# Strassen's seven products for the first block's gate and up products

## The chip, the cores and the metric

The program runs on one core of one Trainium2 chip. The metric is the device time of one execution, in microseconds (us). The engines are TensorE (PE in the profile; PEld are its weight loads), VectorE (DVE), ScalarE (ACT), GpSimd (POOL) and SyncE (SP), which starts the DMAs here.

## The reference

Two transformer-like blocks of depth 2 each, one after the other, on 512 tokens of 1024 features; the first block puts 16 more tokens in front (528). All is float32. What the change touches is the feed-forward part of the first block's two layers, cut here from the reference:

```python
        hn = rms_norm(h, norm_ffn_g[l])
        g, u = jnp.split(hn @ w_gu[l], [D_FF], axis=-1)
        h = h + (jax.nn.silu(g) * u) @ w_down[l]
```

with 1024 features and `D_FF` = 2816. Ahead of it in a layer stands the mixer (attention and a recurrent branch, joined by an output product), behind the second layer stands the second block.

## The kernel before, in words

Features lie on the partitions, in tiles of 128: the residual `h` is 8 tiles of 128 x 528 float32. Nothing is multiplied in plain float32: both operands are split into a high part (rounded to fp32r) and the rest, and a product is three matmuls, high by high, high by low and low by high (`mm3`, L95 to L98). A moving operand in two parts is `xa` (`xh_all`, `xl_all`). A weight tile of 1024 x 128 arrives by DMA as `wraw`; `weight` (L86 to L93) makes `whi` with a ScalarE cast (L90) and `wlo` with a VectorE subtraction (L92), three buffers of each. `split` (L120) does the same for an activation (L121 ScalarE, L122 VectorE).

The feed-forward part of a layer is L571 to L603. `prep` (L256) scales `h` by the norm's gain and writes it to `xa` in two parts (L260 ScalarE, L261 VectorE); the norm's factor per token, `r2`, comes from `sumsq` (L180, adds at L186) and `rnorm` (L153), and is multiplied in after the products. The 22 tiles of gate features and the 22 of up features are done pair by pair, in groups of 8, 7 and 7 pairs (`nf`). A pair is: 8 tiles of K times three matmuls over all the tokens for the gate (`proj`, L111), eviction times `r2` (L588, VectorE), silu (L589, ScalarE), the same for up (L593), their product (L594, VectorE) and its split into `yh` and `yl` (L121, L122). The tokens are two spans of 264 in layer 0 and one of 512 in layer 1, where the 16 extra tokens are no longer needed. After a group, its part of the down product goes through 8 tiles of output features `m`, summed over the group's `nf` tiles, and is added to `h` (L602).

The mixer ends with the output product `w_out` (L551), whose second half (n = 1) is added to `h[m]` for m = 0 to 7 in turn (L561); `prep` follows tile by tile. GpSimd has no instruction in the feed-forward part. In other stages it adds squares and sums (L680, L692), multiplies by rope tables (L401, L652), adds to `h` in the mixer (L559) and squares (L1106).

PSUM is one pool for the whole program: 8 banks, named mm (3), sc (2), tr, av and bc. The framework that builds the program puts each engine's instructions in an order of its own making (ready ones first, by their place in the program), and sets the semaphores; on the chip every engine runs its queue in order.

## Time and profile before

| | us |
|---|---|
| median of 3 runs | 2864.72 |
| lowest, highest | 2864.29, 2868.45 |
| span of the profiled execution | 2861.2 |
| TensorE busy in it | 2781.5 (97%) |
| VectorE busy | 1736.3 (61%) |
| ScalarE busy | 1227.4 (43%) |
| GpSimd busy | 367.0 (13%) |

A page of the profile is read from its first part (busy times) to the chain that ended last (part 4), which says on which engine the time was spent; the granted clock (PEclk) is TensorE's, as a share of its full 2.4 GHz. Matmuls are pipelined: one shows about 0.28 us, though the next starts after 0.12 us, so their cost is the distance between starts. An operation on DVE or POOL shows its own time and any time in which it had started but could not go on.

### The profile page before, as it was taken

The numbers are of one execution on the slowest core, as the hardware profiler recorded it, in microseconds if no ns is written. First come the engines' busy times: TensorE is split into PE (matmuls) and PEld (weight loads), VectorE is DVE, ScalarE is ACT, GpSimd is POOL, SyncE is SP. The second block draws the span as 40 slices with busy tenths as digits, with TensorE's granted clock in tenths as the row PEclk, the third lists the DMA queues.
The fourth block names the chain that finished last, engine by engine and source line by source line (L and its number), as shares of the span: only waits on it lengthen the run. The fifth ranks groups of instructions, "written<-read, shape, count | busy, mean of one in ns | idle before, by whom it ended". The sixth has DMA issues, their size and how long they took to land.

```text
span 2861.2 us, 42993 instructions
## 1 busy us (share of the span) xinstructions
PE 2781.5 (97%) x16548; PEld 2422.5 (85%) x16548; DVE 1736.3 (61%) x3534; ACT 1227.4 (43%) x2174; POOL 367.0 (13%) x403
## 2 busy tenths in 40 slices
PE   8989999999999999999999999999999999999998
PEld 7989999999887888887889888888877898888887
DVE  7887434457888434458977573333789875633335
ACT  6665222235665222235665442332445754433323
POOL 0011000000110000002220031111322110311112
PEclk9999999999999999999999999999999999999999
DMA  4332332332333333336324123333264242233331
GB/s 146 89 79 85 90 89 85 94 89 92 99 85 100 95 92 94 94 95 166 112 82 140 59 81 97 96 96 96 70 155 132 75 136 72 60 106 95 96 96 64
DMA packets 96491, 277.18 MB, mean 97 GB/s; under 512 B 13344, under 2 KB 20000, under 8 KB 96288
## 3 DMA queue, kind: packets, MB, share of 16 engines
q1 hardware_dynamic: 96288, 274.45, 32.7%
q8 instruction: 131, 2.15, 0.3%
q14 instruction: 72, 0.59, 0.1%
HBM read 241.82 MB, written 2.10 MB: 85 GB/s over the span
## 4 chain that ended last, share of the span: by engine, by line
PE 87%; DVE 8%; issue 2%; ACT 2%; POOL 1%; DMA 1%; SPq 0%; ACTq 0%; DVEq 0%; POOLq 0%
PE mm L97 25%; PE mm L98 25%; PE mm L96 25%; PE av L96 1%; PE av L97 1%; PE av L98 1%; PE av L161 1%; DVE wlo L92 1%; PE bc L827 1%; PE av L712 1%; PE tr L827 1%; DVE sq L402 1%; PE bc L176 0%; PE sc L96 0%; PE sc L833 0%
## 5 line engine op out<-in xcount | busy, mean ns | idle before, releaser
L96 PE MATMUL mm<-xh_all,whi 128*128 128x512 f32 (+2 forms) x2752 | 926.0, 338 | 12.4 <-ACT xh_all L260 6.8
L97 PE MATMUL mm<-xl_all,whi 128*128 128x512 f32 (+2 forms) x2752 | 930.3, 339 | 1.4 <-DVE xl_all L745 0.8
L98 PE MATMUL mm<-xh_all,wlo 128*128 128x512 f32 (+2 forms) x2752 | 925.9, 337 | 0.0
L90 ACT CAST whi<-wraw 128x1024 fp32r<-128x1024 f32 (+2 forms) x460 | 465.4, 1013 | 1017.7 <-PE mm L97 823.9
L92 DVE TENSOR_TENSOR wlo<-wraw,whi 128x1024 fp32r<-128x1024 f32 (+2 forms) x437 | 540.7, 1238 | 233.7 <-ACT whi L90 231.7
L96 PEld LDWEIGHTS mm<-xh_all,whi 128*128 128x128 f32 x2752 | 518.8, 189 | 66.6 <-ACT xh_all L260 6.8
L97 PEld LDWEIGHTS mm<-xl_all,whi 128*128 128x128 f32 x2752 | 519.8, 189 | 54.5 <-DVE xl_all L745 1.8
L98 PEld LDWEIGHTS mm<-xh_all,wlo 128*128 128x128 f32 x2752 | 521.0, 189 | 49.8
L1106 POOL TENSOR_TENSOR r<-r 128x512 f32<-128x512 f32 (+1 forms) x70 | 101.9, 1456 | 531.6 <-ACT r L1105 531.6
L97 PE MATMUL mm<-yl,whi 128*128 128x264 f32 (+1 forms) x528 | 169.9, 322 | 0.1
L98 PE MATMUL mm<-yh,wlo 128*128 128x264 f32 (+1 forms) x528 | 169.5, 322 | 0.0
L96 PE MATMUL mm<-yh,whi 128*128 128x264 f32 (+1 forms) x528 | 168.5, 320 | 0.0
L673 DVE TENSOR_TENSOR hall<-hall,mm 128x512 f32<-128x512 f32 (+1 forms) x82 | 46.6, 568 | 145.9 <-PE mm L98 145.9
L593 DVE TENSOR_TENSOR su<-mm,rbc 128x264 f32<-128x264 f32 (+1 forms) x66 | 34.3, 519 | 139.8 <-PE mm L98 139.8
L602 DVE TENSOR_TENSOR hall<-hall,mm 128x264 f32<-128x264 f32 (+1 forms) x72 | 37.1, 515 | 120.6 <-PE mm L98 120.6
L97 PEld LDWEIGHTS mm<-yl,whi 128*128 128x128 f32 x528 | 99.2, 188 | 8.8 <-DVE yl L122 0.6
L96 PEld LDWEIGHTS mm<-yh,whi 128*128 128x128 f32 x528 | 99.0, 188 | 7.6
L98 PEld LDWEIGHTS mm<-yh,wlo 128*128 128x128 f32 x528 | 99.2, 188 | 7.3
L588 DVE TENSOR_TENSOR sg<-mm,rbc 128x264 f32<-128x264 f32 (+1 forms) x66 | 34.0, 517 | 103.2 <-PE mm L98 101.6
L671 DVE SCALAR_TENSOR_TENSOR hall<-hall,mm 128x512 f32<-128x512 f32 x32 | 22.0, 687 | 66.9 <-PE mm L98 66.8
L692 POOL TENSOR_TENSOR accq<-accq,nsq 128x512 f32<-128x512 f32 (+1 forms) x48 | 57.9, 1205 | 25.4 <-ACT nsq L690 24.0
L432 POOL MEMSET vh<- 128x128 f32 x8 | 1.6, 205 | 463.6 <-PE mm L98 414.8
(672 smaller groups left out, 5446.3 us busy)
## 6 DMA issues: line engine op xcount, KB each, us to landing
wraw<-w2f SPq DMA_DIRECT2D x128, 512.0 KB, 3.7
wraw<-w1gu SPq DMA_DIRECT2D x88, 512.0 KB, 3.6
wraw<-w2in SPq DMA_DIRECT2D x44, 512.0 KB, 3.9
wraw<-w1in SPq DMA_DIRECT2D x40, 512.0 KB, 3.7
wraw<-w2mkv SPq DMA_DIRECT2D x32, 512.0 KB, 3.8
wraw<-w1dn SPq DMA_DIRECT2D x32, 448.0 KB, 3.3
wraw<-w1out SPq DMA_DIRECT2D x32, 256.0 KB, 2.7
wraw<-w1dn SPq DMA_DIRECT2D x16, 512.0 KB, 3.5
```

The costliest lines, as they stand in the source:

```text
L90: nc.scalar.copy(hi[:, :kt], raw[:, :kt])
L92: (eng or nc.vector).tensor_sub(lo[:, :kt], raw[:, :kt], f(hi[:, :kt]))
L96: nc.tensor.matmul(ps, wh, xh, start=first, stop=False)
L97: nc.tensor.matmul(ps, wh, xl, start=False, stop=False)
L98: nc.tensor.matmul(ps, wl, xh, start=False, stop=last)
L588: nc.vector.tensor_mul(sg[:, a:b], p, r2[:, a:b])
L593: nc.vector.tensor_mul(su[:, a:b], p, r2[:, a:b])
L602: nc.vector.tensor_add(h[m][:, a:b], h[m][:, a:b], p)
L673: nc.vector.tensor_add(X(m, a, b), X(m, a, b), p)
L692: nc.gpsimd.tensor_add(self.accq[:, a:b], self.accq[:, a:b], sq[:, a:b])
L827: nc.tensor.transpose(ps[:, 128 * j:128 * j + 128], p[:, 128 * j:128 * j + 128], ident)
L1106: nc.gpsimd.tensor_mul(r[:, a:b], r[:, a:b], r[:, a:b])
```

## The change

The products of a pair of weight tiles, `w1` (gate) and `w2` (up), become seven products of quarters in place of eight. The two halves of K (4 tiles each) are one pair of indices, gate and up another, and the first and second half of the tokens the third. `halves4` makes four sums and differences of 4-tile halves of the weights on GpSimd (two tiles of scratch, `s` and `s4`, one buffer each), and splits the seven halves in two parts. The moving side's sums and differences are made once a layer, in the place of `prep` (three GpSimd and one VectorE operation of half the tokens for each of 4 pairs of feature tiles). `seven` runs the products, each 4 tiles of K times three matmuls over half the tokens (264 or 256 columns), and adds them up in four VectorE operations from PSUM to `e`. `r2` is now multiplied in on GpSimd, before and after the silu. The groups are 6, 6, 5 and 5 pairs. The down product goes over the tokens in halves in both layers, with one eviction for both. PSUM is now a pool that is closed and opened anew at the start and the end of each feed-forward part, with three pairs of banks inside it. All else in the diff is comments taken out.

```diff
+    def halves4(pool, w1, w2):
+        r1 = wpool.tile([128, 8, 128], F32, name="wraw", bufs=3)
+        nc.sync.dma_start(r1, w1)
+        r2 = pool.tile([128, 8, 128], F32, name="wraw2", bufs=2)
+        nc.sync.dma_start(r2, w2)
+        s = pool.tile([128, 8, 128], F32, name="ws", bufs=1)
+        s4 = pool.tile([128, 4, 128], F32, name="ws4", bufs=1)
+        nc.gpsimd.tensor_add(s[:, 4:], r2[:, :4], r2[:, 4:])
+        nc.gpsimd.tensor_sub(s[:, :4], s[:, 4:], r1[:, :4])
+        nc.gpsimd.tensor_sub(r2[:, :4], r1[:, :4], r2[:, :4])
+        nc.gpsimd.tensor_sub(s4, r1[:, 4:], s[:, :4])
+        got = []
+        for x in (r1, s, r2, s4):
+            if x is s4:
+                hi = pool.tile([128, 4, 128], F32R, name="wh4", bufs=1)
+                lo = pool.tile([128, 4, 128], F32R, name="wl4", bufs=1)
+            else:
+                hi = wpool.tile([128, 8, 128], F32R, name="whi", bufs=3)
+                lo = wpool.tile([128, 8, 128], F32R, name="wlo", bufs=3)
+            split(hi, lo, x)
+            got += [(hi[:, o:o + 4], lo[:, o:o + 4]) for o in range(0, hi.shape[1], 4)]
+        return got
+    def seven(pool, w, x, n):
+        a11, a12, s2, s1, s3, a22, s4 = w
+        b11, b21, t2, t1, t3, b22, t4 = x
+        def product(ps, w, x):
+            for k in range(4):
+                mm3(ps, w[0][:, k], w[1][:, k], x[0][k], x[1][k], k == 0, k == 3)
+        e = pool.tile([128, 4, n], F32, name="quarters", bufs=2)
+        u = pool.tile([128, n], F32, name="u1", bufs=2)
+        p1 = bank("av")[:, :n]
+        p26, p57, p34 = (pair_of_banks()[:, :, :n] for _ in range(3))
+        product(p1, a11, b11)
+        nc.scalar.copy(u, p1)
+        product(p26[:, 0], a12, b21)
+        product(p26[:, 1], s2, t2)
+        nc.vector.tensor_add(e[:, 0:4:3], p26, twice(u))
+        product(p57[:, 0], s1, t1)
+        product(p57[:, 1], s3, t3)
+        nc.vector.tensor_add(e[:, 1:3], p57, twice(e[:, 3]))
+        nc.vector.tensor_add(e[:, 3], p57[:, 0], e[:, 2])
+        product(p34[:, 0], s4, b22)
+        product(p34[:, 1], a22, t4)
+        nc.vector.tensor_add(e[:, 1:3], p34, e[:, 1:3])
+        return e
...
-                prep(G_FFN, l0, T)
+                half = (T - l0) // 2
+                n0, n1 = slice(l0, l0 + half), slice(l0 + half, T)
+                th, tl = (ff.tile([128, 4, 3, half], F32R, name=n) for n in ("th", "tl"))
+                with tc.tile_pool(name="tq", bufs=1, side="right") as tq:
+                    for k in range(4):
+                        g1, g2 = (tq.tile([128, T], F32, name=n, bufs=1) for n in ("g1", "g2"))
+                        for g, e in ((g1, k), (g2, k + 4)):
+                            nc.scalar.activation(g[:, l0:], h[e][:, l0:], AF.Copy, scale=col(G_FFN + e))
+                        split(xa[k][0][:, n0], xa[k][1][:, n0], g1[:, n0])
+                        split(xa[k + 4][0][:, l0:], xa[k + 4][1][:, l0:], g2[:, l0:])
+                        t = tq.tile([128, 3, half], F32, name="tt", bufs=1)
+                        t3 = tq.tile([128, half], F32, name="t3", bufs=1)
+                        nc.gpsimd.tensor_sub(t[:, 0], g1[:, n1], g1[:, n0])
+                        nc.gpsimd.tensor_sub(t[:, 1], g2[:, n1], t[:, 0])
+                        nc.vector.tensor_sub(t3, g2[:, n1], g1[:, n1])
+                        nc.gpsimd.tensor_sub(t[:, 2], g2[:, n0], t[:, 1])
+                        split(th[:, k], tl[:, k], t)
+                        split(xa[k][0][:, n1], xa[k][1][:, n1], t3)
...
-                for nf in (8, 7, 7):
+                for nf in (6, 6, 5, 5):
...
+                        w = halves4(ff, w1gu[l, 2 * (f0 + i)], w1gu[l, 2 * (f0 + i) + 1])
+                        e = seven(ff, w, rhs, half)
+                        sg, su = (e[:, o:o + 2].rearrange("p a b -> p (a b)") for o in (0, 2))
+                        sl = ff.tile([128, T], F32, name="sl", bufs=1)
+                        nc.gpsimd.tensor_mul(sg, sg, r2[:, l0:])
+                        nc.scalar.activation(sl[:, l0:], sg, AF.Silu)
+                        nc.gpsimd.tensor_mul(sl[:, l0:], sl[:, l0:], r2[:, l0:])
+                        nc.vector.tensor_mul(su, su, sl[:, l0:])
...
                     for m in range(8):
                         w = weight(w1dn[l, m, :, f0:f0 + nf], nf)
-                        for p, a, b in proj(w, ys, late):
-                            nc.vector.tensor_add(h[m][:, a:b], h[m][:, a:b], p)
+                        ps = pair_of_banks()[:, :, :half]
+                        for j, n in enumerate((n0, n1)):
+                            for k, (yh, yl) in enumerate(ys):
+                                mm3(ps[:, j], w[0][:, k], w[1][:, k], yh[:, n], yl[:, n], k == 0, k == nf - 1)
+                        t = h[m][:, l0:].rearrange("p (a b) -> p a b", a=2)
+                        nc.vector.tensor_add(t, t, ps)
                     f0 += nf
+            open_psum("psum_m")
```

## Rows read from the trace of the kernel before

**Rows 1.** The page: busy times, granted clock in 40 slices, chain that ended last.

```profile
PE 2781.5 (97%) x16548; PEld 2422.5 (85%) x16548; DVE 1736.3 (61%) x3534; ACT 1227.4 (43%) x2174; POOL 367.0 (13%) x403
...
PEclk9999999999999999999999999999999999999999
...
PE 87%; DVE 8%; issue 2%; ACT 2%; POOL 1%; DMA 1%; SPq 0%; ACTq 0%; DVEq 0%; POOLq 0%
```

**Rows 2.** Busy time by stretch, the two feed-forward parts: from:to, length, engines, clock, DMA.

```profile
283.00:668.00 385.00, 384.90 (x3155) 384.05 (x3153) 178.63 (x296) 108.43 (x133) 0.67 (x5) 1.00 0.31 92
...
912.00:1269.00 357.00, 357.00 (x1545) 289.53 (x1544) 159.46 (x192) 101.56 (x124) 0.00 (x0) 1.00 0.32 95
```

**Rows 3.** Timeline (start, length): matmuls of 264 (25 apart), 512 (23), 256 (29).

```profile
354.84 0.28 PE L97 MATMUL mm<-xl_all,whi 128*128 128x264 f32 x1
...
357.89 0.28 PE L98 MATMUL mm<-xh_all,wlo 128*128 128x264 f32 x1
...
1119.66 0.39 PE L97 MATMUL mm<-yl,whi 128*128 128x512 f32 x1
...
1124.99 0.39 PE L96 MATMUL mm<-yh,whi 128*128 128x512 f32 x1
...
1275.76 0.28 PE L96 MATMUL mm<-xh_all,whi 128*128 128x256 f32 x1
...
1279.19 0.28 PE L98 MATMUL mm<-xh_all,wlo 128*128 128x256 f32 x1
```

**Rows 4.** Groups by line, VectorE, layer 0: count, busy us, mean ns, idle before.

```profile
L92 DVE TENSOR_TENSOR wlo<-wraw,whi 128x1024 fp32r<-128x1024 f32 x52 | 63.6, 1223 | 19.8 <-ACT whi L90 19.8
...
L594 DVE TENSOR_TENSOR su<-su,sg 128x528 f32<-128x528 f32 x22 | 15.6, 709 | 2.3
L122 DVE TENSOR_TENSOR yl<-su,yh 128x528 fp32r<-128x528 f32 x22 | 15.4, 702 | 0.0
```

**Rows 5.** Lines of GpSimd, and silu: duration ns min/median/max, whole program.

```profile
L559 POOL TENSOR_TENSOR hall<-hall,raw x24: 744/1164/1751, 208.6 to 871.4; 128x264 f32<-128x264 f32 x16, 128x512 f32<-128x512 f32 x8
L680 POOL TENSOR_TENSOR acc<-acc,hall x18: 1272/1294/2116, 1477.7 to 2819.5; 128x512 f32<-128x512 f32 x18
...
L401 POOL TENSOR_TENSOR raw<-raw,ct x16: 1313/1735/2213, 57.4 to 828.4; 128x528 f32<-128x528 f32 x12, 128x512 f32<-128x512 f32 x4
...
L589 ACT ACTIVATE sg<-sg x44: 625/634/645, 285.3 to 1225.3; 128x528 f32<-128x528 f32 x22, 128x512 f32<-128x512 f32 x22
```

**Rows 6.** Timeline: GpSimd and VectorE operations that overlap in time.

```profile
57.38 1.89 POOL L401 TENSOR_TENSOR raw<-raw,ct 128x528 f32<-128x528 f32 x1
57.99 1.83 DVE L402 TENSOR_TENSOR sq<-sq,ct 128x528 f32<-128x528 f32 x1
...
84.02 1.73 POOL L401 TENSOR_TENSOR raw<-raw,ct 128x528 f32<-128x528 f32 x1
84.49 0.43 DVE L396 TENSOR_TENSOR raw<-mm,rbc 128x264 f32<-128x264 f32 x1
...
1477.74 1.29 POOL L680 TENSOR_TENSOR acc<-acc,hall 128x512 f32<-128x512 f32 x1 [1.79 <-DVE hall L671]
1477.76 2.36 DVE L92 TENSOR_TENSOR wlo<-wraw,whi 128x1024 fp32r<-128x1024 f32 x1 [0.16 <-ACT whi L90]
```

**Rows 7.** Timeline, VectorE, the end of layer 0's output product.

```profile
255.44 0.69 DVE L92 TENSOR_TENSOR wlo<-wraw,whi 128x512 fp32r<-128x512 f32 x1
...
265.52 0.42 DVE L561 TENSOR_TENSOR hall<-hall,mm 128x264 f32<-128x264 f32 x1
...
274.61 0.42 DVE L561 TENSOR_TENSOR hall<-hall,mm 128x264 f32<-128x264 f32 x1
```

**Rows 8.** Busy time by stretch, near the start of the program (columns as in Rows 2).

```profile
16.00:18.00 2.00, 0.80 (x6) 0.45 (x4) 1.97 (x4) 2.00 (x3) 0.00 (x0) 1.00 0.00 0
18.00:20.00 2.00, 0.73 (x9) 0.65 (x9) 1.97 (x5) 0.47 (x1) 0.00 (x0) 1.00 0.82 246
...
20.00:30.00 10.00, 9.47 (x56) 8.95 (x56) 7.64 (x36) 2.70 (x5) 0.10 (x1) 0.66 0.54 163
```

More of the change, by code (lines that the diff above doesn't have):

```diff
@@ L52, in both_blocks, with open_psum @@
     res = ctx.enter_context(tc.tile_pool(name="res", bufs=1))
-    psum = ctx.enter_context(tc.tile_pool(name="psum", bufs=1, space=bass.MemoryType.PSUM))
+    banks = ExitStack()
+    psum = None
+    def open_psum(name):
+        nonlocal psum, banks
+        banks.close()
+        banks = ExitStack()
+        psum = banks.enter_context(tc.tile_pool(name=name, bufs=1, space=bass.MemoryType.PSUM))
+    open_psum("psum")
     EARLY = 4
@@ L118, in proj, with twice, pair_of_banks @@
         return got
+    def twice(p):
+        return p[:, None, :].to_broadcast([128, 2, p.shape[1]])
+    def pair_of_banks():
+        return psum.tile([128, 2, 512], F32, name="two", bufs=3)
+    def halves4(pool, w1, w2):
[43 more added lines that the diff above has]
+        return e
     def split(hi, lo, x):
@@ L572, in both_blocks @@
                 share("ff1")
+                open_psum("psum_f")
                 ff = ffn.enter_context(tc.tile_pool(name="ff", bufs=1))
-                prep(G_FFN, l0, T)
+                half = (T - l0) // 2
[16 more added lines that the diff above has]
+                        split(xa[k][0][:, n1], xa[k][1][:, n1], t3)
+                quarters = [[[x[k][:, n] for k in ks] for x in zip(*xa)]
+                            for ks, n in ((range(4), n0), (range(4, 8), n0), (range(4, 8), n1), (range(4), n1))]
+                turned = [[[t[:, k, j] for k in range(4)] for t in (th, tl)] for j in range(3)]
+                rhs = quarters[0], quarters[1], turned[1], turned[0], quarters[3], quarters[2], turned[2]
                 r2 = small.tile([128, T], F32, name="rbc", bufs=1)
@@ L615, in two @@
         return t[:, k:k + 2, a:b]
-    def twice(p):
-        return p[:, None, :].to_broadcast([128, 2, p.shape[1]])
     def products(ms, spans, w, xs, evac):
@@ L636, in phase @@
             close(range(nm - tail, nm), w, xs, evac)
-    with blk2:
+    with banks, blk2:
         def parts(pool, name, shape=None, **kw):
```

14 lines of the change are left out of this document (2 added, 12 removed).

## The prediction

> **What bounds the kernel now.** I read the page first: TensorE is busy 97% of the span, the clock is granted in full, and the chain that ended last is 87% TensorE [rows 1]. Then the busy times by stretch: in the two feed-forward parts TensorE never stops (384.9 of 385 us, 357 of 357), VectorE works 46% and 45% of the time, ScalarE 28%, GpSimd not at all [rows 2]. So this stage is bound by the number of matmuls, and everything else is hidden. The timeline gives their price as the distance between starts: 264 columns 0.122 us (25 steps in 3.05 us), 512 columns 0.232 us (23 in 5.33), 256 columns 0.118 us (29 in 3.43) [rows 3].
>
> **What is removed.** A pair of gate and up tiles took 96 matmuls of 264 columns in layer 0, 11.71 us, or 48 of 512 in layer 1, 11.12 us. It now takes 7 x 4 x 3 = 84 of 264 or 256 columns: 10.25 and 9.94 us. Over 22 pairs that is 32.2 and 26.0 us saved on TensorE. The down product of layer 1 goes from 528 matmuls of 512 columns to 1056 of 256: +2.6 us. TensorE alone would gain 55.6 us.
>
> **What is added, and where it lies.** VectorE was idle for 54% of the time and GpSimd for all of it, so by engine there is room. The question is whether the two can work side by side, and the timeline of other stages answers it [rows 6]. At 1477.74 GpSimd adds for 1.29 us; VectorE's subtraction of the same moment takes 2.36 us, where its kind takes 1.22 [rows 4]: it stood until GpSimd was done. At 57.38 the two alternate: GpSimd's multiply shows 1.89 us for work of 1.31 (its shortest, [rows 5]), VectorE's multiply behind it 1.83 us for 0.71. But at 84.49 VectorE takes its usual 0.43 us beside GpSimd: there one of its two operands is in PSUM. So VectorE operations with both operands in SBUF and GpSimd's two-operand operations take turns on something; I call it the port.
>
> The Trainium skill says the same as a rule (SBUF — State Buffer, Who interferes with whom): the pair of ports that both engines share is an exclusive lock held for the whole instruction, and a VectorE instruction with two SBUF inputs contends with GpSimd reads. By that rule the sum is the one below; without it the sum would be that of the first rival. The 2.36 us above agree with it.
>
> Port work of one pair, layer 0:
> - GpSimd: four weight sums of 512 columns at 1.29 (L680, [rows 5]), 5.16; two multiplies by `r2` of 528 columns at 1.31 (L401), 2.62.
> - VectorE: low parts of `r1`, `s`, `r2` at 1.22 and of `s4` (512 columns) at 0.69 [rows 4, 7], 4.35; `su` 0.71 and `yl` 0.70, 1.41.
>
> Together 13.54 us (layer 1: 13.47, its multiplies being 512 wide). TensorE needs 10.25. Before, the pair's port work was 2 x 1.22 + 1.41 = 3.85 us. The four additions from PSUM do not use the port; no row has their strided or broadcast form, each lies between 0.43 us (264 columns from PSUM, [rows 6]) and twice that, and they can run beside GpSimd. The port is thus the new bound of this stage, unless the stretches around it take up the excess.
>
> **A group of nf pairs.** During the down product the port is nearly free, but buffers limit what can be done ahead: `s` and `s4` have one buffer, `whi` three. Ahead of the group's first matmul fit the first pair's four sums (5.2), three of its four low parts (3.1) and most of two sums of the second pair (2.1): 10.4 us. After the last product may come the last pair's two multiplies, `su` and `yl` (4.0), and all but one multiply of the pair before (2.7): 6.7 us. After the last low part come two more quarter products (24 matmuls, 2.9 us). The port also stands empty at times. Laying the queues out by hand, I find two places in a pair: `yl` waits 0.7 us for its ScalarE cast (0.64, as silu's [rows 5]), and the next multiply waits 0.75 us for the last addition from PSUM. So between 0 and 1.45 us; the order in the queues decides, and I take half, 0.7. From the end of the down product to the last product: 14.24 nf - 14.2 us, that is 71.2 for 6 pairs and 57.0 for 5, against 70.3 and 58.6 before (11.71 each). Layer 1: 70.8 and 56.7 against 66.7 and 55.6.
>
> **The first group of a layer** has no down product in front. `w_out` gives `h[4]` 8.7 us before `h[7]` (three steps of the evictions, 265.5 to 274.6, with 0.4 at the end [rows 7]), and each k of the new preparation needs `h[k+4]`. Its port work per k: three GpSimd differences of 264 at 0.744 (L559, [rows 5]), 2.2; VectorE 0.42 + 0.70 + 0.42 + 0.97 + 0.42 = 2.9 (the 792-column split is interpolated between 0.70 and 1.22). Four of them are 20.6 us; the squares' adds (4 x 0.70) and small operations of the norm make it 24. So from the last eviction to the group's last product: -8.7 + 24 + 6 x 13.54 - 5.9 (first pair's sums and its `s4` part, done earlier) - 6.7 + 2.9 + 4.2 = 91.0 us against 70.3 before (layer 1: 90.6 against 66.7). TensorE stands idle for some 12 us of it.
>
> **The ends of groups.** From the last addition to the last `yl`: 0.7 + 1.31 + 0.64 + 1.31 + 0.71 + 0.64 + 0.70 = 6.0, with a GpSimd or low-part turn in between some 8 us. TensorE can cover it with the other k's of the first two tiles `m` (2 x 30 matmuls, 7.3 us, for 6 pairs; 5.9 for 5): 1.3 us short, eight times, 10.4 us; from 0 (a third `m` started) to 8 each. Reopening PSUM four times: no row shows it; a new bank must wait for its old tile, between nothing and the 3 us of one `m`; I take 0.5 each, 2 us, since the old tiles are evicted in 0.4 to 0.7 us.
>
> **The sum.** Layer 0: 20.7 + 0.9 - 2 x 1.6 = +18.4. Layer 1: 23.9 + 4.1 + 2 x 1.1 = +30.2. Down product +2.6, ends +10.4, PSUM +2. Together +63.6 us on the profiled 2861.2: 2924.8. The median of the runs shown is 3.5 us above the span, so 2928.
>
> **The rivals.**
> 1. *Faster: the turns on the port fall into TensorE's slack, and TensorE stays the bound.* It decides at port work of 10.25 us per pair, for which about a quarter of the 13.54 would have to run side by side, or far more of it be done under the down products. For it: both engines are mostly idle before [rows 1, 2], and there are only 5 or 6 pairs between down products. Against it: [rows 6] show full turns, and one buffer of `s`. Its time: 2864.7 - 55.6 + 2 x 5 for the starts + 2 = 2821.
> 2. *Near no change:* the port binds but never stands empty (-31), the ends are covered (-10.4), half of the starts' excess is hidden by sums made earlier (-20): 2867. For it: the order is made by ready instructions first. Against it: all three at once.
> 3. *Slower still: the order in the queues.* If `yl` stands ahead of the next low part and the multiplies behind the next pair's sums, all 1.45 us are lost: +33, 2961. The clock adds to that: after 4 us with TensorE only 1.5 us busy, the granted clock was 0.66 on average over the next 10 us, between the levels of 2.4 and 1.2 GHz, 3.4 us lost [rows 8]. Waits of some 4 us a pair may bring that back; hidden behind the port in part, half of it in every second pair is 22 x 1.7 = 37 more, 2998.
>
> The Trainium skill (TensorE: Matmul & The Clock Gate, The HAM clock gate) says that the array is throttled by default and that activity releases it; by it the third rival's clock would fall wherever TensorE waits long, and by [rows 1] it never did in the stage as it was.
>
> **How the numbers follow.** Chances: the forecast 0.55, rival 1 0.13, rival 2 0.07, rival 3 0.25. The likeliest is 2928. The range reaches down to rival 2 and up to rival 3 with its clock: 2862 to 3000; it leaves out rival 1 and a little above. A difference of about 0.2% (5.7 us) is what a measurement of this kernel can tell from none. Faster 0.13 (rival 1), same 0.05 (most of rival 2), slower 0.82.
>
> **What the profile of the changed kernel would show.** Right: in the gate and up stretches a pair takes 13.5 to 15 us, TensorE waits there for `whi` or `wlo`; the new 512-column GpSimd sums have a mean well above 1.29 us, and VectorE's 1024-column low parts well above 1.22, since they stand in turns; the sum of their shortest times fills the stretch. The down stretches keep their length, with a short wait at the start of each; a wait of 10 us or more stands at the start of each feed-forward part. Wrong: low parts of 1.22 us beside GpSimd sums of 1.29 that overlap in time, matmuls 0.12 us apart throughout, and pairs of 10.3 us; then the time is rival 1's. If the first groups take 75 us or less, it is the preparation that I have overpriced, and if pairs take 16 us or more with a granted clock under 1, rival 3 holds.

## The result, and the profile after

The changed kernel takes 3006.49 us (median of 4 runs, 3005.14 to 3009.08), the one before 2865.43 us on the same chips (2864.29 to 2868.45): 1.049 times as long [1.0476, 1.0506]. The profiled execution lasts 3003.3 us, 142.1 more than before.

Lines of the page of the changed kernel, to be read against [rows 1]:

```profile
PE 2797.8 (93%) x17604; PEld 2486.8 (83%) x17604; DVE 1917.0 (64%) x3698; ACT 1325.1 (44%) x2356; POOL 792.0 (26%) x691
...
PEclk9998999999999899999999999999999999999999
```

GpSimd works twice as long as before, TensorE stands for 7% of the span, and the granted clock dips in two slices (an 8). The busy times by stretch (columns as in [rows 2]) are the two feed-forward parts with the second layer's mixer between them, and the second block:

```profile
278.00:723.50 445.50, 386.98 (x2922) 375.84 (x2922) 267.32 (x351) 158.35 (x223) 211.49 (x147) 0.94 0.27 82
723.50:969.60 246.10, 232.92 (x1492) 199.67 (x1492) 205.46 (x507) 149.81 (x283) 32.20 (x45) 0.99 0.31 86
969.60:1412.00 442.40, 382.06 (x2916) 371.22 (x2916) 264.12 (x324) 152.47 (x216) 210.65 (x145) 0.93 0.26 80
1412.00:3003.00 1591.00, 1544.07 (x8316) 1303.78 (x8316) 955.54 (x1916) 695.64 (x1311) 301.62 (x291) 1.00 0.33 99
```

Where [rows 2] had TensorE busy for the whole of both feed-forward parts, it is now missing 58 of 445 us and 60 of 442, and the clock is 0.94 and 0.93. By the last evictions of each stage the 142 us lie so: first mixer +3.3, first feed-forward part +56.7, second mixer +8.0, second feed-forward part +74.4, second block -0.2.

The timeline of one pair in the middle of a group (line numbers are each kernel's own; L190 here is `split`'s subtraction), on VectorE and on GpSimd (start, length, and idle time before it with what ended it):

```profile
434.49 0.71 DVE L682 TENSOR_TENSOR quarters<-quarters,sl 128x528 f32<-128x528 f32 x1 [4.56 <-POOL sl L681]
435.11 1.22 DVE L190 TENSOR_TENSOR wlo<-wraw,whi 128x1024 fp32r<-128x1024 f32 x1
...
436.87 0.70 DVE L178 TENSOR_TENSOR quarters<-two,u 128x528 f32<-128x528 f32 x1
437.49 1.22 DVE L190 TENSOR_TENSOR wlo<-ws,whi 128x1024 fp32r<-128x1024 f32 x1
...
441.21 1.69 DVE L190 TENSOR_TENSOR wlo<-wraw,whi 128x1024 fp32r<-128x1024 f32 x1
448.68 0.71 DVE L682 TENSOR_TENSOR quarters<-quarters,sl 128x528 f32<-128x528 f32 x1 [5.77 <-POOL sl L681]
```

```profile
438.83 1.29 POOL L144 TENSOR_TENSOR ws<-wraw 128x512 f32<-128x512 f32 x1 [4.38 <-DVE wlo L190]
440.20 1.62 POOL L145 TENSOR_TENSOR ws<-ws,wraw 128x512 f32<-128x512 f32 x1
441.79 2.26 POOL L146 TENSOR_TENSOR wraw<-wraw,wraw 128x512 f32<-128x512 f32 x1
444.00 1.30 POOL L147 TENSOR_TENSOR ws<-wraw,ws 128x512 f32<-128x512 f32 x1
445.26 1.33 POOL L679 TENSOR_TENSOR quarters<-quarters,rbc 128x528 f32<-128x528 f32 x1
447.34 1.30 POOL L681 TENSOR_TENSOR sl<-sl,rbc 128x528 f32<-128x528 f32 x1 [0.76 <-ACT sl L680]
```

The pair comes round every 14.19 us (14.06 in the second layer). Two things are to be seen. Where both engines have work they alternate: the low part that starts at 441.21 ends 1.08 us after the sum of 440.20 is done (441.82), so it did its work only then, and the sum of 441.79 ends at 444.05, 1.15 us after that low part. And there is a ring, in which each step follows the one before in a queue or waits for it: `su` (L682) at 434.49, low part of `s` until 438.71, GpSimd's first sum at 438.83 (it writes the one buffer of `s`), three more sums and a multiply, silu, second multiply until 448.64, `su` at 448.68. Did the turns or the ring set the 14.19 us? The page cannot tell; the experiments can.

### The profile page after: what moved, and what is told of

Same layout as the page of the kernel before. It is cut to its first block, busy times and chain, and to the rows that moved or that the text cites. A ratio compares the mean times of both kernels' runs of the same rounds, so it can differ in the third digit from the quotient of the medians.

```text
span 3003.3 us, 46137 instructions
## 1 busy us (share of the span) xinstructions
PE 2797.8 (93%) x17604; PEld 2486.8 (83%) x17604; DVE 1917.0 (64%) x3698; ACT 1325.1 (44%) x2356; POOL 792.0 (26%) x691
## 4 chain that ended last, share of the span: by engine, by line
PE 48%; DVE 4%; issue 1%; ACT 1%; POOL 1%; ACTq 0%; POOLq 0%; DVEq 0%
PE mm L106 14%; PE mm L107 13%; PE mm L105 13%; PE av L105 1%; PE av L106 1%; PE av L107 1%; PE bc L917 1%; PE av L802 1%; PE tr L917 1%; DVE wlo L101 0%; PE sc L923 0%; PE sc L924 0%; DVE hall L817 0%; PE sc L105 0%; DVE isc L986 0%
## 5 line engine op out<-in xcount | busy, mean ns | idle before, releaser
L99 ACT CAST whi<-wraw 128x1024 fp32r<-128x1024 f32 (+3 forms) x388 | 375.3, 970 | 606.3 <-PE mm L106 485.4
L105 PE MATMUL mm<-xh_all,whi 128*128 128x512 f32 (+2 forms) x1696 | 587.7, 349 | 15.6 <-ACT xh_all L328 7.4
L106 PE MATMUL mm<-xl_all,whi 128*128 128x512 f32 (+2 forms) x1696 | 589.9, 349 | 1.3 <-DVE xl_all L835 0.8
L107 PE MATMUL mm<-xh_all,wlo 128*128 128x512 f32 (+2 forms) x1696 | 586.9, 347 | 0.0
L101 DVE TENSOR_TENSOR wlo<-wraw,whi 128x1024 fp32r<-128x1024 f32 (+3 forms) x365 | 435.1, 1193 | 205.0 <-ACT whi L99 201.8
L106 PEld LDWEIGHTS mm<-xl_all,whi 128*128 128x128 f32 x1696 | 321.1, 190 | 38.6 <-DVE xl_all L835 1.9
L107 PEld LDWEIGHTS mm<-xh_all,wlo 128*128 128x128 f32 x1696 | 322.0, 190 | 34.6
L105 PE MATMUL two<-yh,whi 128*128 128x264 f32 (+1 forms) x704 | 205.3, 296 | 37.0 <-ACT yh L189 26.7
L107 PE MATMUL two<-yh,wlo 128*128 128x264 f32 (+1 forms) x704 | 204.9, 292 | 0.0
L106 PE MATMUL two<-yl,whi 128*128 128x264 f32 (+1 forms) x704 | 204.7, 292 | 0.0
L682 DVE TENSOR_TENSOR quarters<-quarters,sl 128x528 f32<-128x528 f32 (+1 forms) x44 | 30.8, 701 | 204.9 <-POOL sl L681 204.9
L190 DVE TENSOR_TENSOR wlo<-wraw,whi 128x1024 fp32r<-128x1024 f32 x88 | 127.8, 1452 | 10.4 <-ACT whi L189 10.4
```

What stands on the lines that cost most here:

```text
L99: nc.scalar.copy(hi[:, :kt], raw[:, :kt])
L101: (eng or nc.vector).tensor_sub(lo[:, :kt], raw[:, :kt], f(hi[:, :kt]))
L105: nc.tensor.matmul(ps, wh, xh, start=first, stop=False)
L106: nc.tensor.matmul(ps, wh, xl, start=False, stop=False)
L107: nc.tensor.matmul(ps, wl, xh, start=False, stop=last)
L190: nc.vector.tensor_sub(lo, x, f(hi))
```

## The experiments

Two theories: the *turns* (GpSimd's operations and VectorE's with two SBUF operands exclude each other, and their sum sets the pair) and the *queues* (each engine works in order, and the ring above sets the pair, whether turns are taken or not). Then what the starts, the ends of groups and the reopened PSUM pools cost. The table gives, for the profiled execution of each kernel, the span, then for layer 0 the first group (from the mixer's last eviction to the last addition of products), the second group, one pair inside it and the down product behind it, then both feed-forward parts (FFN) and the second layer's mixer; all from starts and lengths in the timeline. Where an eviction is done in two steps (the last five rows), it counts as ended with VectorE's step; GpSimd's follows 1.4 to 2.3 us later. A time below that has no interval is one execution; repeated executions of one kernel here lie within 3 to 10 us.

| kernel | span | group 1 | group 2 | pair | down 2 | FFN 0 | mixer 1 | FFN 1 |
|---|---|---|---|---|---|---|---|---|
| before (8 and 7 pairs a group) | 2861.2 | 95.0 | 81.9 | 11.69 | 41.2 | 388.5 | 238.1 | 368.0 |
| changed | 3003.3 | 99.7 | 76.8 | 14.19 | 39.1 | 445.2 | 246.0 | 442.4 |
| s_bufs2 | 2986.8 | 98.6 | 74.9 | 13.6 | 37.6 | 434.8 | 246.1 | 438.4 |
| sums_dve | 2965.6 | 91.2 | 71.6 | 13.22 | 39.6 | 427.0 | 247.6 | 421.6 |
| mults_dve | 2901.2 | 88.3 | 65.6 | 11.9 | 35.3 | 393.8 | 246.3 | 390.8 |
| sums_halved | 2895.8 | 86.0 | 64.8 | 11.73 | 35.3 | 388.3 | 246.3 | 390.0 |
| port_free | 2891.5 | 80.3 | 62.1 | 10.1 to 10.7 | 39.0 | 390.8 | 247.5 | 380.0 |
| all_dve | 2872.6 | 83.5 | 61.8 | 9.5 to 11.0 | 35.8 | 380.3 | 246.2 | 375.4 |
| sums_left_out | 2844.4 | 74.3 | 61.4 | 10.24 | 35.4 | 368.1 | 247.8 | 360.9 |
| plain_start | 2986.8 | 88.1 | 76.7 | 14.18 | 39.9 | 435.5 | 246.3 | 432.3 |
| before_banks | 2880.7 | 96.2 | 81.8 | 11.69 | 41.2 | 389.1 | 249.1 | 369.2 |
| own_banks | 3002.4 | 99.6 | 77.5 | | 39.3 | 449.2 | 239.5 | 442.3 |
| m2_down | 2869.2 | 79.0 | 60.0 | | 37.0 | 373.9 | 257.8 | 367.3 |
| early_b | 2866.3 | 77.9 | 60.0 | | 37.0 | 372.8 | 258.1 | 365.6 |
| best | 2871.0 | 80.9 | 60.9 | | 36.3 | 374.9 | 257.5 | 370.2 |
| last_group | 2856.1 | 80.9 | 60.9 | | 36.3 | 376.3 | 237.7 | 371.1 |
| last_group_two | 2861.2 | 77.5 | 60.0 | | 37.0 | 373.1 | 250.1 | 366.5 |

### What sets a pair

**Memsets in GpSimd's place** (port_free).

```diff
-        nc.gpsimd.tensor_add(s[:, 4:], r2[:, :4], r2[:, 4:])
...
+        for d in (s[:, 4:], s[:, :4], r2[:, :4], s4):
+            for _ in range(3):
+                nc.gpsimd.memset(d, 0.001)
...
-                        nc.gpsimd.tensor_mul(sg, sg, r2[:, l0:])
+                        for _ in range(3):
+                            nc.gpsimd.memset(sg, 0.001)
```

> GpSimd's four weight sums and two multiplies of a pair are replaced by three memsets of the same tile each (some 1.6 us for each place, from the 0.52 us that 0.205 and 0.31 us for 128 and 256 columns point to), so GpSimd is as busy as in the changed kernel and everybody waits for it at the same places, but it reads no SBUF operand; the sums and the scale r2 are left out of the result. Theory of the turns (GpSimd and VectorE's operations with two SBUF operands take turns and their sum sets the pair's 14.2 us): nothing takes turns with VectorE, low parts of 1024 columns go back from about 1.5 to 1.22 us, and a pair takes 10.3 to 11 us, near TensorE's 10.2; time 2865 to 2895. Theory of the queues (VectorE stands 4.5 us a pair behind the multiply by silu, which waits for GpSimd's second multiply, and then GpSimd waits for VectorE's low part of s): the same chain is there, VectorE's own work is 4.35 + 2.5 + 1.4 = 8.3 us and the chain of multiply, silu and multiply 4.5, so a pair takes 12.5 to 13 us; time 2940 to 2960.

Measured: 2893.32 us, pairs of 10.1 to 10.7 us. GpSimd and VectorE side by side:

```profile
404.53 3.30 POOL L146 MEMSET ws<- 128x512 f32 x7 [0.65 <-DVE wlo L189]
407.76 0.55 POOL L679 MEMSET quarters<- 128x528 f32 x1
```

```profile
405.70 0.69 DVE L189 TENSOR_TENSOR wl<-ws,wh 128x512 fp32r<-128x512 f32 x1
...
407.60 1.23 DVE L189 TENSOR_TENSOR wlo<-wraw,whi 128x1024 fp32r<-128x1024 f32 x1 [0.26 <-ACT whi L188]
```

VectorE's low parts show their undisturbed 0.69 and 1.22 us beside a busy GpSimd. So it is GpSimd's reading of SBUF that makes VectorE's operations on two SBUF operands wait (a GpSimd operation with one operand was not tried), and the time is the one expected from the turns. One thing keeps this from deciding alone: the build order of the queues came out differently (memsets of two places are interleaved), so the ring was changed as well.

**A second buffer of `s` and `s4`** opens the ring and leaves the port's work as it is (s_bufs2).

```diff
-        s = pool.tile([128, 8, 128], F32, name="ws", bufs=1)
-        s4 = pool.tile([128, 4, 128], F32, name="ws4", bufs=1)
+        s = pool.tile([128, 8, 128], F32, name="ws", bufs=2)
+        s4 = pool.tile([128, 4, 128], F32, name="ws4", bufs=2)
```

> The tiles of the sums s and s4 get two buffers in place of one, so GpSimd's first sum of a pair no longer waits for VectorE's low part of the pair before. Work on the port is unchanged. Turns: in a pair the port has 6 x 1.31 us of GpSimd's and, by the spacing of VectorE's starts (1.13 us for 1024 columns, 0.62 us for 528 and 512), 3 x 1.13 + 3 x 0.62 us of VectorE's, together 13.1 us; a pair stays between 13.1 and 14.2 us, time 2965 to 3006 us. Queues (a ring: low part of s, GpSimd's four sums and first multiply, silu, second multiply, VectorE's multiply, low part of s): the ring is open, GpSimd's own work of 9.1 us and the silu's 0.8 us are the longest chain, a pair takes 10.3 to 11.5 us; time 2880 to 2920 us.

Measured: 2988.63 us, a pair 13.6 us (13.5 in the second layer). GpSimd's first sum now starts beside VectorE's low parts, as intended, and both take longer for it:

```profile
442.83 1.41 POOL L144 TENSOR_TENSOR ws<-wraw 128x512 f32<-128x512 f32 x1 [1.61 <-DMA wraw<-w1gu]
```

```profile
443.01 1.80 DVE L190 TENSOR_TENSOR yl<-quarters,yh 128x528 fp32r<-128x528 f32 x1
```

The turns hold: what was early is given back by standing. The ring itself was worth 0.6 us a pair.

**Only the multiplies, or only the sums, on VectorE** (mults_dve and sums_dve; the second has L144 to L147 on VectorE in the same way).

```diff
-                        nc.gpsimd.tensor_mul(sg, sg, r2[:, l0:])
+                        nc.vector.tensor_mul(sg, sg, r2[:, l0:])
...
-                        nc.gpsimd.tensor_mul(sl[:, l0:], sl[:, l0:], r2[:, l0:])
+                        nc.vector.tensor_mul(sl[:, l0:], sl[:, l0:], r2[:, l0:])
```

> The two multiplies by r2 of a pair go from GpSimd to VectorE (0.7 us each); the four weight sums stay on GpSimd. Turns: work on the port is 4 x 1.29 + 4.35 + 1.41 + 1.41 = 12.3 us and a pair takes 12.3 to 13 us; time 2935 to 2960. Queues: VectorE stands only behind the silu (about 0.9 us) and has 8.3 + 1.4 = 9.7 us of work, some 1 us more where it is stretched; nothing is exchanged with GpSimd in the middle of a pair, and a pair takes 10.6 to 11.6 us; time 2870 to 2910.

> The four weight sums of a pair go from GpSimd to VectorE (0.7 us each there, GpSimd 1.3 to 1.95); the two multiplies by r2 stay on GpSimd. Turns: work on the port falls from 13.5 to 4 x 0.69 + 2 x 1.31 + 4.35 + 1.41 = 11.1 us, and a pair takes 11.2 to 12.2 us; time 2900 to 2935. Queues: VectorE has 8.3 + 2.8 = 11.1 us of its own and still stands about 4 us behind the multiplies on GpSimd, so a pair takes 14.9 to 15.5 us; time 3030 to 3055.

Measured: 2903.01 us with the multiplies moved, pairs of 11.9 us; 2967.44 us with the sums moved, pairs of 13.2. Both pairs lie between the two theories' values. In the first the port is the bound: GpSimd 4 x 1.29 and VectorE, by the spacing of its starts (1.13 us for 1024 columns, 0.62 for 512 or 528), 3 x 1.13 + 5 x 0.62, together 11.65 of 11.9 us. Its rows:

```profile
413.00 2.31 DVE L190 TENSOR_TENSOR wlo<-wraw,whi 128x1024 fp32r<-128x1024 f32 x1
415.23 1.79 DVE L681 TENSOR_TENSOR sl<-sl,rbc 128x528 f32<-128x528 f32 x1
```

```profile
412.47 1.76 POOL L146 TENSOR_TENSOR wraw<-wraw,wraw 128x512 f32<-128x512 f32 x1
414.19 2.28 POOL L147 TENSOR_TENSOR ws<-wraw,ws 128x512 f32<-128x512 f32 x1
```

With the sums moved the port has 10.35 us of work, yet a pair takes 13.2: here the ring is the bound, and the turns lengthen it:

```profile
431.21 3.44 POOL L679 TENSOR_TENSOR quarters<-quarters,rbc 128x528 f32<-128x528 f32 x1 [7.70 <-DVE quarters L185]
```

```profile
431.05 1.21 DVE L190 TENSOR_TENSOR wlo<-wraw,whi 128x1024 fp32r<-128x1024 f32 x1
432.18 0.68 DVE L146 TENSOR_TENSOR wraw<-wraw,wraw 128x512 f32<-128x512 f32 x1
432.78 0.68 DVE L147 TENSOR_TENSOR ws<-wraw,ws 128x512 f32<-128x512 f32 x1
436.77 0.71 DVE L682 TENSOR_TENSOR quarters<-quarters,sl 128x528 f32<-128x528 f32 x1 [3.30 <-POOL sl L681]
```

GpSimd's multiply starts at 431.21 and ends at 434.65, 1.2 us after the last of three VectorE operations in a row (so the turns don't strictly alternate); then silu, second multiply, and VectorE stands for 3.3 us.

**Both multiplies and two sums on VectorE, two sums left** (sums_halved).

```diff
-        nc.gpsimd.tensor_add(s[:, 4:], r2[:, :4], r2[:, 4:])
-        nc.gpsimd.tensor_sub(s[:, :4], s[:, 4:], r1[:, :4])
+        nc.vector.tensor_add(s[:, 4:], r2[:, :4], r2[:, 4:])
+        nc.vector.tensor_sub(s[:, :4], s[:, 4:], r1[:, :4])
...
```

> Both multiplies by r2 and the first two weight sums of a pair go to VectorE, the other two sums stay on GpSimd. Turns: 2 x 1.31 + 3 x 1.13 + 6 x 0.62 = 9.7 us on the port, less than TensorE's 10.24 us; a pair takes 10.3 to 10.8 us, time 2845 to 2865 us. Queues: VectorE's own work is then 11.9 starts' worth, 3 x 1.13 + 9 x 0.62 + 0.34 = 9.3 us, and it stands in order behind the silu and GpSimd's sums for some 2 us: 11.2 to 11.6 us, time 2880 to 2900 us.

Measured: 2897.58 us and 11.73 us a pair. The expectation by turns counted one operation too few (10.3 us, not 9.7) and would still be short: VectorE never idles in these pairs, its 14 operations are 9.9 us by their spacing, and the other 1.8 us it stands, by this sum, behind the two sums on GpSimd. A turn stops not one operation but the whole queue behind it, those from PSUM too.

**Everything on VectorE** (all_dve: the edits of mults_dve and sums_dve together).

> All four weight sums and both multiplies by r2 of a pair go to VectorE; GpSimd has nothing to do in a pair. If GpSimd's turns were the whole cause, nothing is stretched any more and VectorE's own work sets the pair: 3 x 1.13 + 0.34 + 12 x 0.62 = 11.2 us, a pair takes 11.2 to 11.4 us, the ends of groups go back to the 35.4 and 29.6 us without sums; time 2844.4 + 44 x 1.0 = 2888 us (2878 to 2898), which is less than the 2897.6 us with two sums left on GpSimd although VectorE has 1.2 us more work in a pair. If the order of the queues also costs (VectorE standing behind the silu between the two multiplies, 0.9 us): 12.0 to 12.3 us a pair, time 2915 to 2930 us.

Measured: 2874.37 us, less than either expectation; a group of six takes 61.8 us, within 0.4 of the one without any sums. VectorE does 4.2 us more per pair than in the changed kernel, and the pair is some 4 us shorter. From 366 to 500 us (the rest of the first group's down product, the second group and its down product):

```profile
366.00:500.00 134.00, 133.66 (x1093) 133.03 (x1092) 101.84 (x139) 48.57 (x62) 0.00 (x0) 1.00 0.33 101
```

TensorE is busy throughout, VectorE for 76%, and the low parts are back at a mean of 1.22 us. That six pairs stay under six times VectorE's 11.2 us will be because the first pair's share is made beside the down product; no run separates that.

**Without sums and multiplies** (sums_left_out).

```diff
-        nc.gpsimd.tensor_add(s[:, 4:], r2[:, :4], r2[:, 4:])
...
-        for x in (r1, s, r2, s4):
+        for x in (r1, r2, r2, r1[:, 4:]):
...
-                        nc.gpsimd.tensor_mul(sg, sg, r2[:, l0:])
...
-                        nc.gpsimd.tensor_mul(sl[:, l0:], sl[:, l0:], r2[:, l0:])
```

> The four weight sums and the two multiplies are left out of the pair (the sums' places in the seven products get tiles that are already there, r2 isn't applied); all 84 matmuls, splits and additions of products stay. This shows what TensorE's 84 matmuls and the kernel's starts and ends cost alone. If everything that the prediction had mis-sized outside the pair (starts, ends of groups, mixers, together some 55 us) is there without GpSimd too: 2865 to 2885. If these come from GpSimd's share as well: 2815 to 2840. In both a pair takes 10.2 to 10.4 us.

Measured: 2846.18 us. TensorE's saving is as predicted: 22 pairs x (11.69 - 10.24) and x (11.12 - 10.00), 56.5 us. But the span is only 16.8 us under the kernel before. The rest: first groups +11.4 and +13.2 (74.3 - 61.4, less the 1.4 us that the first group has over the others before; 74.4 - 60.0, less 1.25), second mixer +9.7, down products +4.6, first mixer +1.3. So the sums and multiplies, made on GpSimd, cost 3003.3 - 2844.4 = 158.9 us, and 40 us are lost without them.

### Starts, ends and mixers

**The preparation** (plain_start: the scaling and splitting of the kernel before in place of the sums of quarters).

```diff
-                with tc.tile_pool(name="tq", bufs=1, side="right") as tq:
...
+                prep(G_FFN, l0, T)
...
-                rhs = quarters[0], quarters[1], turned[1], turned[0], quarters[3], quarters[2], turned[2]
+                rhs = quarters[0], quarters[1], quarters[2], quarters[3], quarters[3], quarters[2], quarters[1]
```

> The preparation of the operand is the one of the kernel before (hi and lo of the scaled residual, no sums of quarters), and the seven products take plain quarters in place of t1 to t4; so what is left out is the forming of the right operands' sums, and nothing else. If the start is what Strassen's preparation costs, the first group of a layer should last as long as the second one (76.8 and 76.0 us) and some 1.4 us, as the first group of the kernel before does against its others, in place of 99.7 and 101.5 us: time about 2963 us (2955 to 2972). If the preparation costs only what it costs without the other operations on GpSimd (74.3 against 61.4 and 74.4 against 60.0 us, less 1.4 us), and the rest of the first group's excess is the port of the pairs: about 2981 us (2976 to 2990).

Measured: 2988.53 us, as by the second expectation. The first groups shorten by 11.6 and 11.1 us, the price that the run without sums gives for the preparation, and remain 11 and 14 us over the second ones. The changed kernel's timeline shows why. VectorE and GpSimd in the first layer's start:

```profile
282.12 1.19 DVE L207 TENSOR_TENSOR nwt<-nwt,nwv 88x12 f32<-88x12 f32 x1
283.35 0.17 DVE L209 TENSOR_SCALAR nwt<-nwt 88x12 f32<-88x12 f32 x1
...
287.14 2.45 DVE L214 SCALAR_TENSOR_TENSOR nwu<-nwu,nwt 88x12 f32<-88x12 f32 x2
```

```profile
284.61 3.74 POOL L146 TENSOR_TENSOR wraw<-wraw,wraw 128x512 f32<-128x512 f32 x1
```

The operation of L207 in the kernel before, where GpSimd does nothing at this place:

```profile
279.90 0.17 DVE L139 TENSOR_TENSOR nwt<-nwt,nwv 88x12 f32<-88x12 f32 x1
```

The norm's operations of 12 columns take 0.17 us undisturbed; those with two SBUF operands here wait out a whole GpSimd sum, 1.2 us each (L214 is two of them). GpSimd's sum of 284.61 in its turn shows 3.74 us: VectorE does five operations in a row before it. The first pair's sums, which the prediction put into a free stretch, lie among the preparation. TensorE, from the busy times by stretch (columns as above):

```profile
278.00:288.00 10.00, 5.60 (x30) 4.14 (x30) 8.64 (x15) 4.12 (x7) 8.50 (x6) 0.72 0.29 106
288.00:298.00 10.00, 3.80 (x12) 2.49 (x12) 6.78 (x9) 4.82 (x10) 6.53 (x8) 0.50 0.18 52
298.00:308.00 10.00, 8.93 (x58) 8.70 (x59) 9.72 (x8) 4.68 (x6) 7.76 (x5) 0.76 0.17 52
```

It is missing 11.7 of these 30 us, and its granted clock is 0.50, the lower of its two levels (1.2 GHz), through the middle 10 us, and 0.72 and 0.76 on average in the other two.

**The ends of groups** need no run of their own. VectorE's last addition of products and TensorE at the end of the changed kernel's first group, and the last matmuls' stretch with its clock (columns as above):

```profile
377.23 0.71 DVE L185 TENSOR_TENSOR quarters<-two,quarters 128x528 f32<-128x528 f32 x1
...
379.41 0.28 PE L107 MATMUL two<-yh,wlo 128*128 128x264 f32 x1
383.49 0.64 PE L105 MATMUL two<-yh,whi 128*128 128x264 f32 x3 [3.80 <-ACT yh L189]
...
384.87 0.42 PE L107 MATMUL two<-yh,wlo 128*128 128x264 f32 x1
385.09 0.42 PE L105 MATMUL two<-yh,whi 128*128 128x264 f32 x1
...
388.17 0.31 PE L107 MATMUL two<-yh,wlo 128*128 128x264 f32 x1
...
384.87:388.20 3.33, 3.33 (x18) 3.33 (x17) 0.00 (x0) 0.00 (x0) 0.00 (x0) 0.50 0.00 0
```

From 375.32 on 33 matmuls of the down product go ahead, then TensorE stands 3.8 us for the last pair's `yh`, and from 384.87 to 388.17 matmuls start 0.22 us apart in place of 0.12. The granted clock is 0.50 there, the lower level. In the run with the multiplies on VectorE the same waits are 9.7 us for all eight ends, in place of 26.7, and a down product is back to 35.3 us.

**The PSUM pools reopened in the kernel before** (before_banks: the pool closed and opened at the changed kernel's places, nothing else).

```diff
...
                 share("ff1")
+                open_psum("psum_f")
...
                     f0 += nf
+            open_psum("psum_m")
```

> The kernel before with the PSUM pools closed and opened again at the changed kernel's places, ahead of and behind each FFN part, and nothing else. If this accounts for the 8 to 10 us by which the second layer's mixer is longer in the changed kernel and in the one without sums: 2870 to 2876 us. If that lies in the changed order or in which buffers are free: 2863 to 2867 us (2 us for each of up to four places at most).

Measured: 2882.79 us, 19 more than before. The second mixer is 11.0 us longer, the second block 5, the feed-forward parts 0.6 and 1.2. The second mixer, in the kernel before and here:

```profile
663.50:901.60 238.10, 229.22 (x1494) 197.47 (x1493) 203.88 (x500) 146.39 (x276) 31.18 (x46) 1.00 0.32 89
...
665.70:914.80 249.10, 237.68 (x1492) 203.14 (x1492) 203.89 (x500) 148.81 (x278) 29.85 (x45) 0.97 0.30 85
```

Before, TensorE was busy for 229 of its 238 us there at a clock of 1.00, here for 238 of 249 at 0.97: most of the difference is the same matmuls at a lower clock. No wait of this stretch is over 1.5 us, at the reopening or elsewhere. What differs is the order: in TensorE's queue as built, the same matmuls stand in another order through this mixer. That the other order opens the gaps behind which the clock falls is the likeliest reading, not shown.

**The changed kernel with the pools left open** (own_banks).

```diff
-        p26, p57, p34 = (pair_of_banks()[:, :, :n] for _ in range(3))
+        p2, p6, p5, p7, p3, p4 = (bank(n)[:, :n_] for n, n_ in zip(("mm", "mm", "mm", "sc", "sc", "tr"), (n,) * 6))
...
-        nc.vector.tensor_add(e[:, 0:4:3], p26, twice(u))
+        nc.vector.tensor_add(e[:, 0], p2, u)
+        nc.vector.tensor_add(e[:, 3], p6, u)
...
```

> The changed kernel without closing and opening PSUM pools: the seven products take the seven single banks of the pools that are there (one addition for each bank, 0.34 us of VectorE's for 264 columns in place of 0.62 for 528), and a down product has a bank and an eviction for each half of the tokens. If the reopened pools made the mixers longer: the second layer's mixer goes back from 246.0 to 238 or 239 us, time 2990 to 3000 us. If not: mixer 244 to 248 us, time 3000 to 3012 us.

Measured: 3004.66 us. The second mixer is back at 239.5 us, as expected; the time is no shorter, because the second block is 4 us longer (1595.5) and the first feed-forward part, with eight additions a pair in place of four, 4 us as well. So the +8 us of the mixer come with reopening the pools (that it is by the order stays unshown), and each build moves some other stage by up to 5 us (second blocks of 1591 to 1597 us stand in these runs, with not a line of that block changed).

### Can TensorE's saving be had?

Five versions go on from all_dve. **m2_down** takes the second multiply out of the pairs (a token's factor can wait until the down product's eviction, which VectorE multiplies and GpSimd adds to the residual). **early_b** also prepares in the order in which the seven products need their operands, the sums on VectorE. **best** also leaves the pools open, as own_banks. **last_group** and **last_group_two** keep the second multiply in the pairs of a layer's last group (`f0` is 17 there) and return to the eviction in one step behind them, the first with single banks and the pools open (from best), the second with pairs of banks and the pools reopened (from early_b).

```diff
-                        nc.vector.tensor_add(t, t, ps)
+                        if f0 == 17:
+                            nc.vector.tensor_add(t, t, ps)
+                            continue
+                        v = ff.tile([128, 2, half], F32, name="v", bufs=2)
+                        nc.vector.tensor_mul(v, ps, r2[:, l0:].rearrange("p (a b) -> p a b", a=2))
+                        nc.gpsimd.tensor_add(t, t, v)
```

These are the evictions of last_group_two; m2_down and early_b have them without the three lines on `f0`.

> As the run with all of a pair's sums and multiplies on VectorE, but the second multiply by r2 (of a row's scale, which commutes with the down product) moves from the 44 pairs to the 64 evictions of the down products: VectorE multiplies the banks by r2 and GpSimd adds that to the residual. VectorE's work in a pair is 10.6 us against TensorE's 10.24 and 10.0 us; in a down product it has 2 x 0.7 us in 3.6 to 4.3 us. Pair 10.6 to 10.9 us, time 2866 us (2856 to 2876), about the kernel before's. If the last evictions of a group and GpSimd's turns beside them cost more than the multiply did: 2880 to 2895 us.

> As the run with the second multiply at the down products, and the preparation is ordered by what the seven products need: first the four tiles of b11, then the four of b21 and b22, and only then the sums t1 to t4, these on VectorE. If the order of the preparation keeps TensorE waiting in the first group of a layer, the first groups get shorter by 6 to 10 us each: time 2846 to 2856 us, less than the kernel before. If VectorE's whole work of preparation and norm is what has to be done before the first pair ends, the order does nothing: within 4 us of the run without it.

> All that the runs have shown together: sums on VectorE, second multiply by r2 at the down products' evictions, the preparation in the order of the seven products, and the PSUM pools left open with the seven products in single banks. If the second layer's mixer (258.1 us in the run with the early preparation) goes back to 238 or 239 us with the pools left open and the rest stays: 2866.3 - 19.5 = 2847 us of span, time 2850 us (2843 to 2856), some 0.5% under the kernel before. If the eight additions in place of four fill VectorE, or the mixer stays long: 2860 to 2875 us.

> As the run called best, but in the last group of each layer the second multiply by r2 stays in the pair (on VectorE) and the down products are added to the residual in one step. If the two-step eviction held up the next stage (TensorE busy for 14.4 of the first 20 us of the second layer's mixer, where it was 20.0 with one step), the mixer goes back from 257.5 to 239 to 246 us, the five pairs of the last groups lose 0.6 us each: span 2871.0 - 12 to -18 + 6 = 2859 to 2865, time 2860 to 2867 us, no more than 0.2% from the kernel before. If it did not: 2873 to 2879 us.

> As the run with the early preparation (pools reopened, pairs of banks), with the same return to the one-step eviction in the last group of each layer. If the two-step eviction held up the next stage, the mixer goes back from 258.1 to 246 us: span 2866.3 - 12 + 6 = 2860, time 2858 to 2864 us. If not: 2870 to 2876 us.

Measured, against the kernel before on the same chip: m2_down 2873.96 us, 1.0027 [1.0017, 1.0037]; early_b 2871.76, 1.0017 [1.0007, 1.0026]; best 2872.79, 1.0021 [1.0012, 1.0030]; last_group_two 2863.23, 0.9993 [0.9984, 1.0002]; last_group 2857.90, **0.9973 [0.9964, 0.9982]**. Against what was expected, m2_down and last_group_two lie in their first range, early_b and best in their second, and last_group 2 us under its first. Moving the multiply brought the groups to 60.0 us, as hoped, but the second mixer went to 258 us and took most of it; the order of the preparation is worth 1 to 2 us a layer, not 6 to 10. Leaving the pools open, which was to bring the mixer back, left it at 257.5 us (best). With the last group's eviction in one step the mixer is 237.7 us with the pools open (last_group), but 250.1 with them reopened (last_group_two), so both had lengthened it. The stretches of last_group's feed-forward parts and second mixer:

```profile
275.70:652.00 376.30, 364.83 (x2923) 360.06 (x2922) 328.26 (x573) 163.55 (x224) 45.24 (x53) 0.99 0.31 97
652.00:889.70 237.70, 229.07 (x1495) 197.46 (x1493) 202.01 (x500) 147.32 (x283) 31.18 (x44) 1.00 0.31 87
889.70:1260.80 371.10, 359.02 (x2917) 353.75 (x2918) 329.87 (x559) 158.80 (x218) 43.76 (x52) 0.98 0.32 98
```

So Strassen's form can beat the kernel before, by 0.3%: of the 56.5 us that TensorE saves 5 remain in the span and 8 in the medians. That is no more than stages move from build to build, and last_group_two is level with the kernel before. The first layer's feed-forward part is 12 us shorter, the second's 3 us longer (371.1 against 368.0): TensorE saves less there (24.6 us of 56.5), and its first group is 82.4 us where six pairs at TensorE's pace are 60.

## Why the prediction was wrong in size

The direction was right, and so in the main was the mechanism, the turns on the port; the size was 63.6 us where 142.1 came. The step that failed most is the group's credit for work made ahead, and every term for a start or an end was too low:

- **TensorE's saving**, 32.2 + 26.0 us: right (56.5 by the run without sums). The second layer's down product, put at +2.6, is 4.4 us longer in that run.
- **The turns on the port**: right. The Trainium skill (SBUF — State Buffer, Who interferes with whom) adds that GpSimd instructions which only write do not contend; the memsets agree, with 1.22 us for the low parts beside them.
- **The pair's 14.24 us**: measured 14.19, but by luck, since two terms were off and cancelled. The port's work is 13.0, not 13.5: a start follows the one before after 1.13 or 0.62 us, though its row shows 1.22 or 0.70. That leaves 1.15 us in which the port stands empty, not 0.7, and not at the two places that were laid out: in the pair shown it is empty while GpSimd's second multiply waits 0.76 us for the silu, and during VectorE's addition from PSUM at 436.87, while GpSimd still waits for the one buffer of `s`. The second buffer took 0.6 us away.
- **Group time "14.24 nf - 14.2"**: this is the step that failed most. Measured is 14.19 nf - 8.4. A group of six is 10.25 + 4 x 14.19 + 9.8 = 76.8 us: of the 10.4 us put for sums and low parts made ahead the first pair saves 3.9, since it can't be faster than TensorE, and what was made ahead beyond that is not carried to the second pair. Nor did a second buffer carry it (74.9 at 13.6 a pair). The last pair saves 4.4 us, where 6.7 - 2.9 = 3.8 was put. Over the six groups of 5 or 6 pairs that stand behind others this is 31 us (400.4 measured, 369.4 predicted).
- **The first groups**, 91.0 and 90.6 us: 99.7 and 101.5 measured, 19.5 us more in all. The miss lies ahead of the first pair's last addition: it ends 32.9 and 36.3 us after the mixer's last eviction, where the terms put (-8.7 + 24 - 5.9 + 14.2) give 23.6; from there the pairs follow as in the other groups. The 12 us of TensorE's idle time were right (11.7), but they are many waits of 2.7 us at most in the first layer, and beside them the clock was down, which had no term. The price of the preparation alone is 11 to 13 us a layer. Not seen was that the first pair's sums, "done earlier", would be done among the preparation and stretch the norm's small operations. How the miss divides between these and the clock is not shown. (`h[4]` comes 9.1 us before `h[7]` by the rows, not 8.7.)
- **The ends of groups**, 1.3 us each: 4.1 us measured (the down products last 144.4 and 142.0 us in the two layers, their 1056 matmuls 128.8 at 0.122 and 124.6 at 0.118; the 33 us between are eight ends). The chain was estimated at 6 to 8 us, which holds (the last addition starts at 377.23, TensorE goes on at 383.49). The cover failed: TensorE had 33 matmuls ahead, one tile `m` and three matmuls, not two tiles with 60; and the clock fell behind the wait. The down products together are 34.4 us longer than before, where 13.0 was put (10.4, and 2.6 for the second layer's): 21 us.
- **PSUM reopened**, 0.5 us four times: the mixers are 11.3 us longer. The 8.0 us of the second come with reopening, by own_banks; it was priced as a wait for old tiles, and no wait over 1.5 us stands in the longer mixer of before_banks. The 3.3 us of the first stay open: the runs with reopened pools have -0.1 to +4.3 us there.

The sum of these, 31 + 19.5 + 21 + 9, is the missing 78.5 us but for 2. Of the signs, those of a pair came (14.19 us; GpSimd's four sums with means of 1.35 to 1.95 us); a wait of 10 us at the start and down stretches of the old length did not. **Rival 3** came nearest in time (2961 to 2998, with 3006 measured), but not by its road: its pair of 13.54 + 1.45 = 15.0 us was not there. Its clock was: 0.94 and 0.93 in the feed-forward parts, for which TensorE's same matmuls are busy for 387.0 and 382.1 us in place of 361.7 and 354.9 without GpSimd's work; a part of that lies where TensorE would have waited anyway, so it is no term to be added. **Rival 1** needed port work in TensorE's slack; with all of it on VectorE (all_dve) the pairs come close to its 10.25 us, and the time is still 2874, since it put 10 us for the starts and 2 for PSUM, where first groups 22 us over the second ones and a mixer of +8 us stand.

## What to carry to other kernels

Before work goes to an idle GpSimd, count what it and VectorE read from SBUF together: moved back to the "busier" VectorE, the same six operations made the kernel 132 us faster, because each takes half the time there (0.68 us against 1.29) and a turn of GpSimd's stops VectorE's whole queue (some 1.8 us a pair with two sums left). The Trainium skill (Perfetto Trace Analysis, Optimizing Scalar/DVE Operations) warns that offloading between these two might not help; here it cost 132 us. And a saving in the steady state has to pay for each start and end: with 8 groups and 2 preparations, 56 us of matmuls bought 5 of the span in the best build.

## What the runs showed of the hardware

- An operation that has the port kept it to its end here. Mostly the two engines alternated, but a GpSimd multiply of 1.3 us showed 3.44 behind three VectorE operations in a row and a sum of 1.29 us 3.74 behind five; what decides is open. A VectorE operation of 0.17 us showed 1.2 beside GpSimd's sums. GpSimd's memsets took no turn (low parts of 0.69 and 1.22 us beside them).
- The same sum of 512 columns takes 1.29 us on GpSimd and 0.68 on VectorE, so moving it to VectorE also halves its time on the port.
- A wait of TensorE of 3.8 us was followed by 1.4 us of matmuls 0.12 us apart and then 3.3 us of matmuls 0.22 us apart, with a granted clock of 0.50 (1.2 GHz).
- The same program with its PSUM pool closed and opened four times had a mixer 11 us longer, with the same matmuls in another order; a difference of 10 us between two builds of a kernel need not lie where the edit is.
